# The second up projection of a gated decoder layer as two blocks of seven products, with sums of its weights kept in DRAM

## The chip, the core and the metric

The kernel runs on one core of one Trainium2 chip. Its engines are PE (TensorE, matrix products and transposes), DVE (VectorE), ACT (ScalarE), POOL (GpSimd) and SP (SyncE); each takes its own instructions in order, and they wait for each other by semaphores. DMA transfers are issued here from SP (weights, and the result) and from POOL (everything else); PEld in the profile is the loading of a matmul's stationary operand. The metric is the device time of one execution in microseconds (us), lower is better. All arithmetic is float32. A product of two float32 matrices is made on PE of three passes, by splitting each operand into a high part (a rounded copy, made on ACT) and a low part (operand minus high part, made on DVE): high x high, high x low, low x high.

## The reference, cut to what matters

The sequence has 512 rows, the model 2048 columns. One layer of a decoder trunk:

```python
h = rms_norm(x, norm_g[l])
proj = h @ w_in[l]
q, kv, g_logits, z_a, uv, z_b, merge_logits = jnp.split(proj, SPLIT_IDX, axis=-1)
...
o_a = nsa_attention(q, k_c, v_c, k_s, v_s, k_w, v_w, g_logits, ...) * jax.nn.silu(z_a)
o_b = spatial_gating(uv, ln_v_g[l], ln_v_b[l], sgu_w[l], sgu_b[l]) * jax.nn.silu(z_b)
g_a, g_b = jnp.split(jax.nn.sigmoid(merge_logits), 2, axis=-1)
merged = g_a * (o_a @ w_up_a[l]) + g_b * (o_b @ w_up_b[l])
x = x + merged @ w_out[l]
x = x + jax.nn.sigmoid(x @ w_ple_gate[l]) * (p[l] @ w_ple[l])
return rms_norm(x, final_g)
```

`o_a` and `o_b` are 512 x 1024, `w_up_a` and `w_up_b` are 1024 x 2048. The change is about `o_b @ w_up_b`.

## The kernel before

**Jobs.** Every product with a weight matrix is a `Job` (line 39); the function `gemm` (line 331) runs all jobs in the order in which they were added and hands control back after each small unit of matmuls, so that other work can be put between units (`fill(n)` runs n units, `finish(name)` runs to the end of a job). There are three kinds. "T" has the weights as the stationary operand (four blocks of 128 rows to a piece of weights, 12 matmuls). "N" has the activations as the stationary operand and makes a block of 512 columns from all rows of weights. "S" makes a block of 1024 columns and all 512 rows by seven products of half-size blocks instead of eight (the scheme of Strassen in Winograd's form): the seven products are named 1, 5, 6, 3, 7, 2 and 4, and sums and differences of quarter blocks stand for the operands of 5, 6, 7 and 4 on the weight side, and of 5, 6, 3 and 7 on the activation side. Weight sums are made on DVE in `sum_to` (line 245, the subtract at L258), results are added up in `evac_quad` (line 672): products 1, 5 and 6 are copied out of PSUM by ACT (`keep`), products 3, 7 and 2 are added to these by DVE, product 4 is passed on directly.

**Order of the jobs.** pl0 to pl3; kc0, kc1, vc0, vc1, k00, k01, k10, k11 (kind T, four pieces each), vs (N, 256 columns, eight pieces), vw (N, 304 columns, sixteen pieces), then eight q and eight za jobs around the attention, u, vn, zb (S), the merge gates m0 to m3 (S), ua0 and ua1 (S, `o_a @ w_up_a`), ub0 to ub3 (N, `o_b @ w_up_b`, line 807), wo0, wo1 (N) and wo2 (S), pg0, pg1, pg3.

**Weights on their way.** A piece goes through `load_to` (SP, into a ring of tiles: three for `raw`), a copy on ACT (`hi` or, for kind S, `hs`, 128 x 1024) and a subtract on DVE (`lo` or `ls`), both from `split_to` (line 270), which runs two pieces ahead of PE; the rings of `lo`, `hs` and `ls` have three tiles. At every piece `pop` (line 324) also runs `state["pops"]` steps of the queue `background`, a list of small functions. What has been put into `deferred` is run at the next piece.

**Beside the keys and values.** `h_chunk` (line 455) makes sums of the normalized input and stores them (`hsum`, POOL) from k01 on, half a step per piece. The memory of the ring `b11` (four tiles) is free from kc0 until the first q job takes tiles of it; two of the four hold weights of the compressor for a while.

**Beside the gates.** During m0 to m3 the background queue first finishes a layer norm: `ln_load`, `ln_affine` (two DVE instructions, L1535 and L1536, for each of eight blocks of 128 rows x 512 columns, through DRAM and a pair of tiles `v`), then eight times `group` (line 539): load the operands (`first`, `second`), a spatial product on PE six steps later, its gate on DVE, a transpose on PE (`turn`), a split, and two stores to `ob_dram`.

**The up projections.** ua takes its seven activation operands ("slots", 1 MB each) from DRAM, where `oa_chunk` (line 1386) has stored sums of `o_a` with their high and low parts. Its results go to the tiles `h` of the activation memory. The gate of the first branch is loaded to the tiles `l` (`load_gate_a`) and multiplied in by `gate_a` (DVE, L791) during ub. ub reads `o_b` from two tiles of 2 MB. `evac_up` (line 794) multiplies by the second gate (DVE, L798) and adds the first branch (POOL, L800). `turn_merged` (line 1639) then transposes the merged block on PE, eight transposes at a time, and splits it for the output projection.

Of the kernel before, what the change touches and what calls it, by code (L numbers as in the profile page):

```python
# [37 lines left out]
class Job:  # L38
# [8 lines left out]
    def __init__(self, name, kind, w, c0, cols, kt, act, evac, banks=None, tail=0, c2=None, order=("15", "63", "7", "24")):  # L47
# [3 lines left out]
        self.order = order  # L51
# [13 lines left out]
def kernel(ctx: ExitStack, tc: tile.TileContext, x, p, norm_g, w_in,  # L65
# [59 lines left out]

    def act_part(i, k, sl):
        if isinstance(k, slice):
            return parts_of[i][k.start // 4][:, k.start % 4:k.start % 4 + k.stop - k.start, sl]
        return parts_of[i][k // 4][:, k % 4, sl]
# [50 lines left out]
    def add_job(job):  # L180
        jobs.append(job)
        if job.kind == "S":
            half, c2 = job.kt // 2, job.c2
            ld = {}
            direct = job.order[0] == "1"
# [28 lines left out]
    state = {"loads": 0, "sum": 0, "high": 0, "low": 0, "ahead": 0, "more": 1, "pops": 2, "due": 0, "b11": 0}  # L214
# [30 lines left out]
    def sum_to(i):  # L245

        while state["sum"] <= min(i, len(subs) - 1):
            job, p, j, ld = subs[state["sum"]]
            if job.kind != "S" or p not in "5674":
                state["sum"] += 1  # L250
                continue
# [8 lines left out]
    def source(i):  # L260
        job, k, n, ld = subs[i]
        if job.kind == "S":
# [60 lines left out]

    def pop():
        state["due"] += state["pops"]
# [207 lines left out]
    def evac_q(ft):  # L533
        def f(ps):
            pair = ring((0, 3, 2)[ft % 3], F32R)
# [71 lines left out]
    ob_dram = dram.tile([P, 2, 8, S], F32R, name="ob_d")  # L607
# [140 lines left out]
    def ob_act(k):  # L748
        return ob_h[:, k], ob_l[:, k]

    oa_slot = {}

    def oa_act(p, k, t):
        return (oa_slot[p][:, i, k, t * P:t * P + P] for i in range(2))
# [13 lines left out]
    up_tiles = {}  # L768

# [6 lines left out]
    def load_gate_b(cg):  # L776
        up_tiles[cg] = new_s4(cg - 1, F32) if cg in (1, 2) else new_x()
        nc.gpsimd.dma_start(up_tiles[cg], gate_columns(1, cg))
# [15 lines left out]
    def evac_up(cg):  # L794
        def e(ps):
            g = up_tiles[cg]
            for t in range(TT):
                nc.vector.scalar_tensor_tensor(out=g[:, t], in0=g[:, t], scalar=1.0, in1=ps[t],  # L798
                                               op0=ALU.add, op1=ALU.mult)
                nc.gpsimd.tensor_tensor(out=g[:, t], in0=g[:, t], in1=parts_of["h"][cg][:, t], op=ALU.add)  # L800
        return e

    for i in range(2):
        add_job(Job(f"ua{i}", "S", w_up_a, 1024 * i, 512, 8, oa_act, evac_quad(None, lambda t, c, i=i: place_up_a(t, 1024 * i + c)),
                    (("o", "t", "s"), ("g", "t", "s"))[i]))
    for cg in range(4):
        add_job(Job(f"ub{cg}", "N", w_up_b, 512 * cg, 512, 8, ob_act, evac_up(cg), (ys, xs)[cg % 2]))
# [207 lines left out]
    quad["ring"] = ph_r.enter_context(tc.tile_pool(name="ring", bufs=1))  # L1015
    mid = ph_ab.enter_context(tc.tile_pool(name="mid", bufs=1))
# [369 lines left out]
    def oa_chunk(c):  # L1386

        w = {}

        def load():  # L1390
            for n, f in (("1", c), ("2", c + 4)):
                w[n] = mix["pool"].tile([P, S], F32, tag="v", name="oa_f", bufs=2)
                nc.gpsimd.dma_start(w[n], o32_dram[:, f])

        def put(n, tags, places, sl=slice(0, 512)):

            def f():
                width = sl.stop - sl.start
                h = mix["pool"].tile([P, S], F32R, tag=tags[0], name="oa_" + tags[0])
                if len(tags) == 2:  # L1400
                    l = mix["pool"].tile([P, S], F32R, tag=tags[1], name="oa_" + tags[1])
                else:
                    l = w[n].bitcast(F32R) if width == 512 else h[:, 256:]
                high(h[:, :width], w[n][:, sl], 0.5)

                def rest():
                    low(h[:, :width], l[:, :width], w[n][:, sl], 0.5)
                    for j, i in enumerate(places):
                        for a, o in enumerate((h, l)):
                            nc.gpsimd.dma_start(oa_dram[:, i, a, c], o[:, 256 * j:256 * j + 256])  # L1410
# [8 lines left out]
        def sums_24():  # L1419
            f1, f2 = w["1"], w["2"]  # L1420
            sub(f1[:, lo_t], f2[:, hi_t], f1[:, lo_t])
            sub(f2[:, lo_t], f2[:, lo_t], f1[:, lo_t])

# [81 lines left out]
    def load_s3():  # L1505
        for q in range(2):
# [126 lines left out]
    for cg in range(3):  # L1633
        load_gate_b(cg)
# [236 lines left out]
```

## Time and profile before

| | us |
|---|---|
| median of three runs | 1551.98 (1551.78 to 1552.4) |
| the profiled execution, its own time | 1551.81 |
| its span, first to last instruction | 1550.1 |
| PE busy | 1536.1 (99%) |
| DVE busy | 1194.6 (77%) |
| ACT busy | 785.4 (51%) |
| POOL busy | 251.4 (16%) |

| Stage | from, to (us) | length |
|---|---|---|
| keys and values, kc0 to vw | 32.3 to 181.4 | 149.1 |
| gates m0 to m3 | 720.0 to 1036.1 | 316.1 |
| ua | 1036.1 to 1112.3 | 76.2 |
| ub, with three of four `turn_merged` | 1112.3 to 1204.7 | 92.4 |

How to read the profile: it is one execution as the hardware profiler recorded it. A row of a group gives line, engine, operation, the names it writes and reads, shapes, count, then busy us and mean ns of one, then the idle time before it and what ended that. A row of the timeline gives start, duration, engine, line, operation, and in brackets the idle time before it and its releaser. In the list of waits a row gives the waiting instruction, the one that released it, us in total, times, and the longest. The rows themselves stand in the prediction.

### The profile page before, as it was taken

The page shows a single profiled execution, that of the slowest core. Times are in us where ns is not written, and L with a number is a line of the kernel's source. Part 1 is how long each engine was busy: PE and PEld are TensorE (multiplying, and loading weights), DVE is VectorE, ACT ScalarE, POOL GpSimd, SP SyncE. Part 2 cuts the span into 40 slices and gives each one's busy share as a digit, 9 for nine tenths or more (in the row PEclk, how much of TensorE's full clock was granted, in tenths as well). Part 3 has the DMA queues.
Part 4 walks back from the last instruction along what each step waited for, and adds up shares of the span by engine and source line. Part 5 has one row for each costly group of instructions (what it writes and reads, how often), then busy time and mean ns, then how long its engine had stood idle before and what let it go on. Part 6 is the DMA issues. An engine that isn't in the chain of part 4 may idle for free.

```text
span 1550.1 us, 20517 instructions
## 1 busy us (share of the span) xinstructions
PE 1536.1 (99%) x7438; PEld 1287.8 (83%) x7438; DVE 1194.6 (77%) x1869; ACT 785.4 (51%) x1345; POOL 251.4 (16%) x413
## 2 busy tenths in 40 slices
PE   9999999999999999999999999999999999999997
PEld 7889988888888888888888888888888888888886
DVE  7547758888886888978887777777666587888877
ACT  6434446666675555545545444455423344544556
POOL 1201101101122242201121212210131221000000
PEclk9999999999999999999999999999999999999999
DMA  8436722123226895826473737674743497464655
GB/s 322 129 82 195 224 71 59 49 61 107 78 69 212 251 294 133 265 69 230 144 258 116 262 104 254 233 259 175 289 132 96 120 278 228 150 203 165 189 202 192
DMA packets 161429, 269.23 MB, mean 174 GB/s; under 512 B 9752, under 2 KB 80048, under 8 KB 158768
## 3 DMA queue, kind: packets, MB, share of 16 engines
q1 hardware_dynamic: 116240, 151.67, 31.1%
q0 software_dynamic: 44944, 116.00, 22.3%
q8 instruction: 58, 0.95, 0.2%
q14 instruction: 43, 0.35, 0.1%
q10 hardware_dynamic: 144, 0.26, 0.0%
HBM read 209.69 MB, written 58.20 MB: 173 GB/s over the span
## 4 chain that ended last, share of the span: by engine, by line
PE 96%; DVE 2%; ACT 1%; issue 0%; POOL 0%; DVEq 0%; POOLq 0%; ACTq 0%
PE ps_m L355 7%; PE ps_m L357 7%; PE ps_m L356 7%; PE ps_za L381 2%; PE ps_t L1204 2%; PE ps_za L382 2%; PE ps_za L383 2%; PE ps_ub L393 2%; PE ps_ub L394 2%; PE ps_wo L394 2%; PE ps_ub L395 2%; PE ps_wo L395 2%; PE ps_wo L393 2%; PE ps_wo L356 2%; PE ps_wo L355 2%; PE ps_pg L356 2%
## 5 line engine op out<-in xcount | busy, mean ns | idle before, releaser
L148 DVE TENSOR_TENSOR ls<-b,hs 128x1024 fp32r<-128x1024 f32 x196 | 239.7, 1224 | 116.1 <-ACT hs L142 115.0
L142 ACT CAST hs<-b 128x1024 fp32r<-128x1024 f32 x196 | 206.1, 1052 | 231.3 <-PE ps_m L357 88.0
L148 DVE TENSOR_TENSOR lo<-raw,hi 128x512 fp32r<-128x512 f32 (+1 forms) x216 | 151.6, 706 | 81.8 <-issue 26.1
L142 ACT CAST hi<-raw 128x512 fp32r<-128x512 f32 (+1 forms) x216 | 129.3, 606 | 138.6 <-PE ps_ub L395 48.5
L142 ACT CAST hs<-raw 128x1024 fp32r<-128x1024 f32 x80 | 84.2, 1054 | 98.4 <-PE ps_m L357 35.5
L148 DVE TENSOR_TENSOR ls<-raw,hs 128x1024 fp32r<-128x1024 f32 x80 | 97.8, 1222 | 17.2 <-ACT hs L142 17.0
L355 PE MATMUL ps_m<-hs,act_h 128*128 128x512 f32 x256 | 100.5, 393 | 0.0
L356 PE MATMUL ps_m<-ls,act_h 128*128 128x512 f32 x256 | 99.7, 389 | 0.0
L357 PE MATMUL ps_m<-hs,act_l 128*128 128x512 f32 x256 | 99.7, 389 | 0.0
L258 DVE TENSOR_TENSOR b<-raw,b 128x1024 f32<-128x1024 f32 x80 | 97.5, 1218 | 1.6 <-DMA raw<-in_w_in_dram 1.6
L258 DVE TENSOR_TENSOR b<-b,b 128x1024 f32<-128x1024 f32 x80 | 97.5, 1218 | 0.0
L142 ACT CAST pth<-ps_t 128x512 fp32r<-128x512 f32 (+1 forms) x88 | 48.0, 545 | 65.8 <-PE ps_t L1204 65.4
L1165 ACT ACTIVATE prob<-prob,st 128x512 f32<-128x512 f32 (+3 forms) x128 | 70.7, 556 | 4.0 <-DVE st L1156 3.8
L148 DVE TENSOR_TENSOR ptl<-ps_t,pth 128x512 fp32r<-128x512 f32 (+1 forms) x88 | 56.2, 639 | 21.0 <-ACT pth L142 20.0
L1156 DVE CUSTOM_DVE_ANT_0 prob<-ps_s,b 128x512 f32<-128x512 f32 (+3 forms) x128 | 56.3, 486 | 9.9 <-PE ps_s L1153 9.7
L357 PEld LDWEIGHTS ps_m<-hs,act_l 128*128 128x128 f32 x256 | 48.1, 188 | 10.1
L356 PEld LDWEIGHTS ps_m<-ls,act_h 128*128 128x128 f32 x256 | 48.1, 188 | 9.7
L355 PEld LDWEIGHTS ps_m<-hs,act_h 128*128 128x128 f32 x256 | 48.1, 188 | 9.7
L381 PE MATMUL ps_za<-act_h,hi 128*128 128x512 f32 x128 | 55.7, 435 | 0.0
L381 PE MATMUL ps_q<-act_h,hi 128*128 128x512 f32 x128 | 53.6, 419 | 0.0
L1204 PEld LDWEIGHTS ps_t<-ident,prob 128*128 128x128 f32 x320 | 39.7, 140 | 13.8 <-DVE ptl L148 2.8
L1204 PE MATMUL ps_t<-ident,prob 128*128 128x128 f32 x320 | 49.5, 273 | 1.4 <-DVE ptl L148 1.3
(641 smaller groups left out, 4391.3 us busy)
## 6 DMA issues: line engine op xcount, KB each, us to landing
raw<-in_w_in_dram SPq DMA_DIRECT2D x112, 512.0 KB, 3.8
b<-in_w_in_dram SPq DMA_DIRECT2D x56, 512.0 KB, 5.8
raw<-in_w_out_dram SPq DMA_DIRECT2D x24, 512.0 KB, 4.1
raw<-in_w_ple_gate_dram SPq DMA_DIRECT2D x24, 512.0 KB, 3.9
raw<-in_w_up_b_dram SPq DMA_DIRECT2D x16, 512.0 KB, 3.7
hsum<-h_stage POOLq DMA_DIRECT2D x12, 512.0 KB, 4.0
gate<-keep POOLq DMA_DIRECT2D x24, 256.0 KB, 4.1
oa_d<-oa_g POOLq DMA_DIRECT2D x40, 128.0 KB, 3.1
```

Of the source, the lines that this page charges most:

```text
L142: nc.scalar.copy(hi, src)
L148: nc.vector.tensor_tensor(out=lo, in0=src, in1=hi.bitcast(F32), op=ALU.subtract)
L258: nc.vector.tensor_tensor(out=b[o], in0=b[x], in1=b[y], op=ALU.subtract)
L355: nc.tensor.matmul(o, ah, wh, start=st, stop=False, skip_group_check=go)
L356: nc.tensor.matmul(o, ah, wl, start=False, stop=False, skip_group_check=go)
L357: nc.tensor.matmul(o, al, wh, start=False, stop=sp, skip_group_check=go)
L381: nc.tensor.matmul(ps, hi[:, j], ah, start=st, stop=False)
L393: nc.tensor.matmul(o, ah[:, sl], hi[:, j], start=st, stop=False)
L394: nc.tensor.matmul(o, ah[:, sl], lo[:, j], start=False, stop=False)
L395: nc.tensor.matmul(o, al[:, sl], hi[:, j], start=False, stop=sp)
L1165: nc.scalar.activation(sl, sl, AF.Exp, bias=st[:, 0, j, hh:hh + 1], scale=-1.0, accum_out=st[:, 1, j, hh:hh + 1])
L1204: nc.tensor.transpose(b[:, (2 * e + hh) * P:(2 * e + hh + 1) * P], pts[hh][:, c:c + P], ident)
```

## The change

The four ub jobs become two of kind S of 1024 columns each. Unlike the other jobs of this kind, their weight sums are not made while they run: a new argument `sums` names four DRAM tensors for each block, and every product loads its own weights (`raw`, 512 KB for two blocks of 128 rows).

```diff
+            if job.sums:
+                for p, j in products(job):
+                    c, k = {"1": (job.c0, 0), "2": (job.c0, half), "3": (c2, half)}.get(p, (0, 0))
+                    src = weights(job, k + 2 * j, 2, c) if p in "123" else job.sums[p][:, 2 * j:2 * j + 2]
+                    ld[p, j] = add_load("raw", src, 2, job.cols)
+                    last_sub[ld[p, j]] = len(subs)
+                    subs.append((job, p, j, ld))
+                return
...
-    for cg in range(4):
-        add_job(Job(f"ub{cg}", "N", w_up_b, 512 * cg, 512, 8, ob_act, evac_up(cg), (ys, xs)[cg % 2]))
+    for i in range(2):
+        add_job(Job(f"ub{i}", "S", w_up_b, 1024 * i, 512, 8, slot_act(ob_slot), evac_quad(final_up(i), tiles=False),
+                    (("o", "t", "s"), ("g", "t", "s"))[i], sums=up_sums[i]))
```

The sums are made in eight sets of five steps from kc1 on, in two tiles of the ring `b11`. `pop` runs 0.85 of a step of this new queue `slow` for every piece, ahead of the background's.

```diff
     def pop():
+        state["late"] += 0.85
+        if state["late"] >= 1:
+            state["late"] -= 1
+            if slow:
+                slow.popleft()()
...
+    ab, cd = (ring(i, F32) for i in range(2))
+    def up_set(i, k):
+        a, b, c, d = ab[:, 0], ab[:, 1], cd[:, 0], cd[:, 1]
+        def minus(o, x, y, p):
+            nc.vector.tensor_tensor(out=o, in0=x, in1=y, op=ALU.subtract)
+            nc.gpsimd.dma_start(up_sums[i][p][:, k], o)
+        def load():
+            for o, f, col in ((a, k, 0), (b, k, 512), (c, k + 4, 512), (d, k + 4, 0)):
+                nc.gpsimd.dma_start(o, w_up_b[f * P:f * P + P, 1024 * i + col:1024 * i + col + 512])
+        def first():
+            minus(b, b, a, "5")
+            minus(c, c, b, "6")
+        def second():
+            minus(a, c, a, "7")
+            minus(d, d, c, "4")
+        return [load, lambda: None, first, second, lambda: None]
+    for i in range(2):
+        for k in range(4):
+            slow.extend(up_set(i, k))
```

Beside the gates, `o_b` is now prepared as `o_a` was: two groups make a pair, ACT copies each transposed group to a tile, and then sums of the two are made, split and stored in 14 transfers of 128 KB a pair (`put`, moved out of `oa_chunk` into `put_steps`). The background runs at 1.42 steps a product instead of 1.

```diff
+    def group_pair(c):
+        both = {}
+        put, sums_13, sums_24 = put_steps(both, c, ob_dram, None)
+        def sums_put():
+            sums_24()
+            put("1", ("g0",), (2, 4))()
+        return (group(c, both) + group(c + 4, both) + [nothing, put("2", ("g0", "g1"), (5, 6)), nothing, nothing,
+                put("1", ("v",), (0,), lo_t), sums_13, sums_put, nothing, put("2", ("g1",), (3, 1)), nothing])
...
-    for g in range(8):
-        background.extend(group(g))
-    state["pops"] = 1
+    for c in range(4):
+        background.extend(group_pair(c))
+    state["pops"] = 1.42
```

In the up projections the first gate of columns 0 to 1023 is multiplied in during ua1, that of the others during ub0; seven slots of 1 MB are loaded for ub, five in ua1 and two at its end; the second gate goes to the tiles `l`. The merged block stays in the tiles `h`, and `turn_merged` runs once for two blocks of 512 columns, the second of them first; its results take the places of gates and merged columns that are done with, in pairs of 128 rows that a new table `pair_of` finds again.

```diff
+    def final_up(i):
+        def f(t, c, o, src):
+            cg = 2 * i + c // 512
+            g, m = (parts_of[n][cg][:, t] for n in "lh")
+            nc.vector.scalar_tensor_tensor(out=g, in0=g, scalar=1.0, in1=src, op0=ALU.add, op1=ALU.mult)
+            nc.gpsimd.tensor_tensor(out=m, in0=m, in1=g, op=ALU.add)
+        return f
...
+    state["pops"] = 1
+    gates_a((0, 1))
     load_gate_a(2)
     fill(4 * 4)
-    nc.gpsimd.dma_start(ob_h, ob_dram[:, 0])
+    for i in range(2):
+        load_ob(i, ob_h[:, 4 * i:4 * i + 4])
+    load_gate_a(3)
     fill(4 * 4)
-    nc.gpsimd.dma_start(ob_l, ob_dram[:, 1])
-    load_gate_a(3)
+    for i in range(2):
+        load_ob(2 + i, ob_l[:, 4 * i:4 * i + 4])
+    fill(4 * 2)
+    load_ob(4, new_s4(0))
     finish("ua1")
+    load_ob(5, new_s4(1))
+    load_ob(6, new_x(F32R))
+    gates_a((2, 3))
+    for cg in range(2):
         load_gate_b(cg)
...
+    finish("ub0")
+    assert not background
+    for cg in range(2, 4):
+        load_gate_b(cg)
+    fill(8)
+    turn_merged(0, "oo", 6)
+    finish("ub1")
+    fill(4)
+    turn_merged(1, "gs", 4)
```

Outside of these, four loads of `s3_dram` become eight of half the size.

147 lines of the change are left out of this document (74 added, 73 removed).

## The prediction

> **What bounds the kernel now.** I read the page first (span, engines, slices, chain), then the list of who waited on PE, then busy time by stage, then the order of single instructions where the change adds work.
>
> ```profile
> span 1550.1 us, 20517 instructions
> PE 1536.1 (99%) x7438; PEld 1287.8 (83%) x7438; DVE 1194.6 (77%) x1869; ACT 785.4 (51%) x1345; POOL 251.4 (16%) x413
> ...
> PE 96%; DVE 2%; ACT 1%; issue 0%; POOL 0%; DVEq 0%; POOLq 0%; ACTq 0%
> ...
> PE ps_spin L947 <- POOL eps_t L87: 1.4, 1, 1.4
> PE ps_t L1204 <- DVE ptl L148: 1.3, 1, 1.3
> ```
>
> PE is busy for 99% of the span, holds 96% of the chain, and its two longest waits are 1.4 and 1.3 us. So a matmul taken away shortens the kernel by the spacing of matmuls, and a microsecond for which PE is made to wait lengthens it by as much. The spacing comes from the stages. The columns after the length are busy us (instructions) of PE, PEld, DVE, ACT, POOL, then clock, DMA share, GB/s; the rows are ua, ub, the gates m0 to m3, the keys from k00 on, vs, vw, and three pieces of m0.
>
> ```profile
> 1036.10:1112.30 76.20, 76.20 (x338) 63.10 (x337) 57.85 (x57) 38.70 (x48) 6.79 (x11) 1.00 0.61 221
> 1112.30:1204.70 92.40, 92.40 (x434) 77.05 (x433) 55.02 (x73) 26.70 (x46) 21.86 (x17) 1.00 0.42 138
> 720.00:1036.00 316.00, 315.99 (x1441) 262.44 (x1441) 252.32 (x250) 154.38 (x180) 62.48 (x106) 1.00 0.60 200
> 80.80:131.90 51.10, 51.10 (x251) 42.92 (x251) 30.56 (x55) 22.11 (x40) 1.68 (x4) 1.00 0.39 113
> 131.90:154.90 23.00, 23.00 (x193) 22.99 (x192) 17.20 (x29) 9.70 (x20) 2.65 (x5) 1.00 0.64 190
> 154.90:181.40 26.50, 26.50 (x194) 26.50 (x193) 22.83 (x42) 12.86 (x28) 4.26 (x8) 1.00 0.76 222
> ...
> 720.00:740.00 20.00, 20.00 (x90) 16.54 (x90) 18.50 (x23) 11.96 (x16) 5.37 (x10) 1.00 0.45 153
> 740.00:760.00 20.00, 20.00 (x90) 16.58 (x89) 17.08 (x18) 9.27 (x10) 4.20 (x8) 1.00 0.48 148
> 760.00:780.00 20.00, 20.00 (x90) 16.57 (x89) 18.62 (x21) 11.82 (x14) 2.53 (x6) 1.00 0.63 208
> ...
> L1645 PE MATMUL ps_m<-ident,s 128*128 128x128 f32 x32 | 4.1, 272 | 0.0
> L1645 PE MATMUL ps_m<-ident,x 128*128 128x128 f32 x16 | 2.1, 272 | 0.0
> ...
> 1145.99 0.87 PE ps_m L1645 x8
> ```
>
> ua has the new form of product already: 2 blocks of 7 products of 24 matmuls are 336 in 76.2 us, 0.2268 us each. ub's 384 would take 87.1 us at that spacing, and its six groups of eight transposes 6 x 0.88 = 5.3; the sum is the 92.4 us measured. So ub has no stall to give back, and the duration of 0.39 us that the page shows for one matmul is not its price.
>
> **1. The products.** ub becomes 2 x 7 x 24 = 336 matmuls of the same shape. 48 fewer x 0.2268 = **-10.9 us**. The 64 transposes stay, in eight groups as before.
>
> **2. The sums of the weights, beside keys and values.** Eight sets, each of four loads, four subtracts on DVE and four stores of 256 KB, are issued step by step: 0.85 step for each weight piece, five steps to a set (load, nothing, two subtracts, two subtracts, nothing). 40 steps take 47 pieces, from kc1 into vw. A piece lasts 2.72 us for keys (12 matmuls) and 1.65 in vw (26.5 / 16).
>
> ```profile
> 108.11 0.69 DVE L438 TENSOR_TENSOR h_b<-act_h,act_l 128x512 f32<-128x512 f32 x1
> 108.72 0.69 DVE L438 TENSOR_TENSOR h_a<-act_h,act_l 128x512 f32<-128x512 f32 x1
> ...
> 125.99 0.69 DVE L148 TENSOR_TENSOR lo<-raw,hi 128x512 fp32r<-128x512 f32 x1
> ...
> 171.66 0.47 DVE L148 TENSOR_TENSOR lo<-raw,hi 128x304 fp32r<-128x304 f32 x1
> ...
> 126.74 0.50 PE L383 MATMUL ps_k<-act_h,lo 128*128 128x512 f32 x1
> ...
> 174.92 0.30 PE L394 MATMUL ps_vw<-lo,act_h 128*128 128x304 f32 x1
> ...
> DMA to landing us min/median/max: 2.3/3.0/7.2
> ...
> oa_f<-o_d POOLq DMA_DIRECT2D x8, 256.0 KB, 3.6
> ```
>
> A subtract of this shape takes 0.61 to 0.69 us (starts 0.61 apart), so 32 of them are some 20 us of DVE. From 80.8 to 181.4 DVE is busy 70.6 of 100.6 us, so on average they fit. What counts is DVE's lead: the split-off low part of a piece must be ready when PE comes to it. In vw the part ready at 172.13 is used at 174.92 at the latest, a lead of 2.7 us; at 126.68 one is ready as PE asks for it, and that matmul takes 0.50 us: the lead there is nil already.
>
> The new wait: a subtract waits for its loads, the loads wait on POOL until the set before is stored. By the rows for 256 KB (the first line is the landing of the o_d transfers, min/median/max) that chain is 3.0 for the store, two POOL issues of 0.55, and 3.6 for the load: 7.7 us. Four steps lie between, 4.7 pieces: 12.8 us in the keys, where it is covered, but 7.8 in vw, of which the other subtract takes 0.65. So in vw each of two sets comes late by 0.5 us at medians, and by some 2 more where POOL must first issue an hsum store that waits for DVE, and where the DMA share of 0.76 is raised: a set moves 2.1 MB in 9.8 us, 214 GB/s on top of 222. DVE has 3.7 us idle in vw and gets four pairs, 5.2 us. Queued behind a waiting subtract are the low parts of the next pieces, and PE waits for those. Two sets x (2.5 late + 0.75 of work that does not fit) less the lead of 2.7 is 3.8 us; with 0.7 for the places without lead, **+4.5 us**. From below, 0.5 (the lead covers vw); a gain is excluded, as nothing is removed here. From above, the chain at the longest landings, 7.2 + 1.1 + 7.2 = 15.5 us: priced under the rivals. I take the value near the medians because both transfers have rows of their own size.
>
> **3. Beside the gates.** Per pair of groups of ob DVE gets 1.5 more splits (0.68) and four half-size sums (half of 0.69), 2.4 us; four pairs make 9.7 us on 252.3 of 316 (83% after). ACT's 3.5 more copies a pair and POOL's 40 more stores (0.54 each, 21.6 us) lie on engines busy 154 and 62 of 316. The background runs at 1.42 steps a product instead of 1. That squeezes the layer norm's eight row blocks (1.5 us each, L1535 and L1536) from 26 products into 18, where DVE is already busy 54.2 of 60 us: 12 us of work over 50 instead of 71 raises 90% to about 97%.
>
> ```profile
> 741.99 0.75 DVE L1535 SCALAR_TENSOR_TENSOR v<-v,small,lg 128x512 f32<-128x512 f32 x1
> 742.77 0.75 DVE L1536 SCALAR_TENSOR_TENSOR v<-v,small,lg 128x512 f32<-128x512 f32 x1
> ...
> 746.85 0.54 POOL L1531 DMA_DIRECT2D v<-vn_d  x1 [2.48 <-DMA vl_d<-v]
> ...
> v<-vn_d POOLq DMA_DIRECT2D x8, 256.0 KB, 5.5
> mix_u<-u_d POOLq DMA_DIRECT2D x8, 256.0 KB, 4.7
> ```
>
> A block's buffer comes back by store and load: 741.99 to 746.85, plus 5.5, is 10.4 us; five steps are now 3.5 products, 9.6 us. DVE so waits 0.8 us for the last block of each half, inside a lead of some 3 us (below). **+0.5 us**, from 0 to 3. The operands of the spatial product have 4.2 products (11.5 us) instead of 16.3 to land, against 4.7 and three issues; between pairs a store goes ahead, about 3 us more. No charge; PE would stand behind it directly, up to 3 us.
>
> **4. The ub stage itself.** DVE: 32 low parts of 0.69 go, 28 of 1.22 and 12 sums of 0.64 come, eight gate products of ua move to ua1: 55.0 - 22.1 + 34.2 + 7.7 - 7.1 = 68 of 81.5 us, 83%; the gates run at 80% without a wait of PE.
>
> ```profile
> 1100.01 1.22 DVE L148 TENSOR_TENSOR ls<-b,hs 128x1024 fp32r<-128x1024 f32 x1 [0.31 <-ACT hs L142]
> ...
> 1104.35 0.39 PE L356 MATMUL ps_ua<-ls,x 128*128 128x512 f32 x1
> ...
> raw<-in_w_up_b_dram SPq DMA_DIRECT2D x16, 512.0 KB, 3.7
> b<-in_w_up_a_dram SPq DMA_DIRECT2D x8, 512.0 KB, 8.2
> ...
> L800 POOL TENSOR_TENSOR s<-s,act_h 128x512 f32<-128x512 f32 x8 | 11.9, 1514 | 26.0 <-DVE s L798 26.0
> ...
> 1040.00:1060.00 20.00, 20.00 (x90) 16.58 (x89) 14.96 (x15) 10.72 (x14) 1.60 (x3) 1.00 0.98 371
> ```
>
> The lead in this form is 3.1 us (ready 1101.23, used 1104.35). SP loads 28 pieces of 512 KB, one per 2.72 us, instead of 16. A ring of three gives each about two products plus the lead, 5.8 + 3.1 = 8.9 us, against landings of 3.7, or 8.2 under load. In ub0 come two slots and two gates besides, some 300 GB/s; 371 ran in ua without a stall. POOL's seven slot loads wait in order for PE to leave ua's slots, and the third and fourth gate load stands behind them, needed a job later. After ub1 four POOL adds (6.1 us) end near 7.8 us; the first transposes, after 2.7 us, use the other columns, and those that need the adds come after 9.9. DVE's low parts wait there for the gate tile, about 3.4 us, ahead of a weight piece that PE wants 10.8 us after ub1. **+0.3 us**, from 0 to 3.4.
>
> **Sum.** -10.9 + 4.5 + 0.5 + 0.3 = -5.6 us on the profiled execution: its span of 1550.1 becomes 1544.5, its time of 1551.81 becomes 1546.2. The median of the runs lies 0.17 higher, so I forecast **1546.3 us**.
>
> **Rivals.** (a) All of the new work is hidden: 1551.98 - 10.9 = 1541.1. For it: 30% of DVE is idle beside the keys; against it, the lead of nil at 126.7 and the 0.5 us by which the chain misses in vw even at medians. Chance 0.13.
>
> (b) Slower: the chain of store, issue and load in the keys and values. At 15.5 us vw would lose 2 x (15.5 - 7.15) - 2.7 = 14 us, and five sets in the keys and vs 3.3 us each, less some 2 of lead, 6.5; 1541.1 + 20.5 = 1561.6. It eats the gain from a chain of about 14 us: 2 x (14 - 7.15) - 2.7 = 11. For it: the longest landing, 7.2. Against it: the medians are half of that and most sets run where the DMA share is 0.39 to 0.64. Chance 0.11.
>
> (c) The weight stream in ub is late: landings like 10.8 (two 1 MB gate loads beside 8.2 for the weights) would cost some 2 us at three or four pieces, so 6 more than the forecast: 1552. Against it: ua at 371 GB/s. Chance 0.09. The Trainium skill, DMA: Bandwidth & Descriptors, section "Queues, rings and completion order", says that each DMA engine takes turns between the queues that have work, packet by packet. By that rule SP would keep half of 371 GB/s, 186, beside POOL's four transfers of 1 MB, where the weights need 193 (512 KB in 2.72 us): less than 1 us behind after the 23 us that those 4 MB take, inside the lead, and (c) rarer still.
>
> (d) Waits of PE that lower its clock.
>
> ```profile
> 1540.00:1550.00 10.00, 0.49 (x3) 0.07 (x1) 4.62 (x9) 3.79 (x7) 0.00 (x0) 0.77 0.55 210
> ```
>
> In the last 10 us PE works for 0.49 and the granted clock has a mean of 0.77, so it falls when PE stands still; at half speed that is 4.6 us, a loss of 2.3 us had there been matmuls. Two such falls after waits in vw would add 4.6: 1550.9. Against it: every wait estimated above is under 3 us, and the waits of 1.4 us now cost no clock. Chance 0.05. The Trainium skill, TensorE: Matmul & The Clock Gate, section "Why this matters for your kernels", warns against idle gaps of PE of more than about 3 us, after which the clock goes to half; the row of the last 10 us agrees, and by that rule the waits in vw would stay just short of it.
>
> **How the numbers follow.** The forecast, waits of 2 to 8 us in all (1543 to 1549), has 0.62; (a) 0.13, (c) 0.09, (d) 0.05, (b) 0.11. 0.2% of the time, 3.1 us, is what can be told from no change: faster is under 1548.9, slower over 1555.1. Faster: (a) and nearly all of the forecast, 0.73; same: the rest of it, (c), (d), 0.16; slower: (b), 0.11. The range runs from (a) to just over (c), 1540.8 to 1553.
>
> **What would show it.** 7390 matmuls instead of 7438, ub some 10.9 us shorter with PE still at spacing 0.2268; waits of PE on low parts between 120 and 185 us of 3 to 6 us in all, most of them in vw, with DVE released by the landing of w_up_b. Wrong would be: waits of over 1 us in ub or the gates, no wait before 185 us (a), or several of over 2 us there (b).

## The result, and the profile after

| | before | after |
|---|---|---|
| median of the runs, us | 1551.95 (1551.78 to 1552.4, 4 runs) | 1564.68 (1564.28 to 1566.14, 4 runs) |
| span of the profiled execution, us | 1550.1 | 1562.9 |
| start to the first matmul of za | 203.2 | 220.9 (+17.7) |
| from there to the first of ub | 909.1 | 909.9 (+0.8) |
| ub, to the first matmul of wo | 92.4 | 84.6 (-7.8) |
| wo to the end | 345.4 | 347.5 (+2.1) |

The ratio is 1.0083 (95%: 1.0066 to 1.0101): slower by 12.7 us, where a gain of 5.6 us had been forecast. The stages add up to the 12.8 us by which the span grew. The first place to look is the stretch up to za. It holds keys, values and the first q job, and in it PE has the same matmuls as before.

A line of the page after with the busy times, then two of its DMA issues (count, KB each, median us from issue to landing):

```profile
PE 1535.5 (98%) x7390; PEld 1283.2 (82%) x7390; DVE 1244.4 (80%) x1933; ACT 805.8 (52%) x1369; POOL 317.8 (20%) x526
...
b<-in_w_up_b_dram POOLq DMA_DIRECT2D x32, 256.0 KB, 6.0
t<-b POOLq DMA_DIRECT2D x32, 256.0 KB, 3.7
```

7390 matmuls, 48 fewer, as forecast; the loads of the sums land in 6.0 us and their stores in 3.7, where the forecast had taken 3.6 and 3.0. The list of waits after (waiting instruction, releaser, us in total, times, longest):

```profile
PE ps_vw L416 <- DVE lo L153: 6.9, 2, 4.7
PE ps_ub L378 <- DVE ls L153: 2.3, 4, 1.0
PE ps_k L405 <- DVE lo L153: 2.1, 1, 2.1
...
PE ps_q L405 <- DVE lo L153: 1.1, 1, 1.1
...
DVE b L1041 <- DMA b<-in_w_up_b_dram: 16.6, 7, 5.2
```

PE waits for low parts, at two places in vw, one in the keys, one in q; DVE, which makes them, waits 16.6 us for the loads of the sums. These PE waits on low parts ahead of za are 10.1 us of the 17.7. Windows of the timeline show most of the rest (length, then busy us and count of PE, PEld, DVE, ACT, POOL, then clock, DMA share, GB/s):

```profile
130.00:135.00 5.00, 5.00 (x16) 3.92 (x16) 4.56 (x8) 1.66 (x3) 0.00 (x0) 0.66 1.04 368
170.00:175.00 5.00, 4.00 (x17) 3.77 (x17) 4.96 (x10) 1.93 (x4) 2.41 (x5) 0.66 0.79 257
185.00:190.00 5.00, 2.45 (x10) 2.45 (x11) 4.24 (x8) 0.00 (x0) 2.17 (x4) 0.51 0.64 219
190.00:195.00 5.00, 5.00 (x31) 5.00 (x31) 4.66 (x10) 3.43 (x7) 1.08 (x2) 0.81 0.93 266
```

Behind each longer wait the granted clock is low for a while. PE's busy time times what the clock lacks, summed over the four rows (1.7 + 1.4 + 1.2 + 0.9), is an estimate of 5.2 us. The chain itself, for the eighth set in vw, DVE's rows and then POOL's:

```profile
171.46 0.68 DVE L1041 TENSOR_TENSOR b<-b 128x512 f32<-128x512 f32 x1
...
179.70 0.47 DVE L153 TENSOR_TENSOR lo<-raw,hi 128x304 fp32r<-128x304 f32 x1
185.32 0.69 DVE L1041 TENSOR_TENSOR b<-b 128x512 f32<-128x512 f32 x1 [5.15 <-DMA b<-in_w_up_b_dram]
```

```profile
171.84 1.14 POOL L1042 DMA_DIRECT2D t<-b  x2 [0.45 <-DVE b L1041]
174.75 0.54 POOL L488 DMA_DIRECT2D hsum<-h_stage  x1 [1.77 <-DVE h_stage L153]
177.19 0.55 POOL L488 DMA_DIRECT2D h_d<-h_stage  x1 [1.90 <-DVE lo L153]
178.06 2.15 POOL L1046 DMA_DIRECT2D b<-in_w_up_b_dram  x4 [0.33 <-issue]
```

The seventh set's last subtract is done at 172.1. POOL has issued its last two stores at 173.0, then has to issue two stores of the h sums, each of which waits for DVE, and comes to the eighth set's loads at 178.06. How long the two stores (`t`, 171.8 to 173 us) and the first two of these loads (`b`, to 178.9 us) took to land:

```profile
DMA to landing us min/median/max: 5.6/5.6/5.6
```
```profile
DMA to landing us min/median/max: 5.5/6.1/6.6
```

So the stores landed at 177.4 and 178.0, just before POOL came to the loads: the h sums ahead of them in its order cost 0.6 us at most. The second load, which the first subtract needs, landed at 185.3; DVE has stood at the subtract for 5.15 us, no low part is made after 180.2, and PE waits 4.7. From subtract to subtract the chain took 13 us. The seventh set's loads, at 161.9, waited 2.25 us for stores that took 5.8 and 5.9 to land.

### The profile page after: what moved, and what is told of

It is laid out like the page before. It is cut to its first block, busy times and chain, and to the rows that moved or that the text cites. A ratio compares the mean times of both kernels' runs of the same rounds, so it can differ in the third digit from the quotient of the medians.

```text
span 1562.9 us, 20745 instructions
## 1 busy us (share of the span) xinstructions
PE 1535.5 (98%) x7390; PEld 1283.2 (82%) x7390; DVE 1244.4 (80%) x1933; ACT 805.8 (52%) x1369; POOL 317.8 (20%) x526
## 4 chain that ended last, share of the span: by engine, by line
PE 83%; DVE 5%; DMA 5%; issue 3%; ACT 2%; POOL 1%; DVEq 0%; POOLq 0%; ACTq 0%
PE ps_m L378 6%; PE ps_m L379 6%; PE ps_m L377 6%; PE ps_za L403 2%; PE ps_t L1248 2%; PE ps_za L404 2%; PE ps_za L405 2%; PE ps_wo L416 2%; PE ps_wo L417 2%; PE ps_wo L415 2%; PE ps_pg L378 2%; PE ps_wo L378 2%; PE ps_zb L378 2%; PE ps_vn L379 2%; PE ps_zb L379 2%
## 5 line engine op out<-in xcount | busy, mean ns | idle before, releaser
L147 ACT CAST hs<-raw 128x1024 fp32r<-128x1024 f32 x108 | 113.6, 1054 | 130.3 <-PE ps_m L379 28.2
L153 DVE TENSOR_TENSOR ls<-raw,hs 128x1024 fp32r<-128x1024 f32 x108 | 139.2, 1290 | 36.2 <-ACT hs L147 36.1
L153 DVE TENSOR_TENSOR lo<-raw,hi 128x512 fp32r<-128x512 f32 (+1 forms) x184 | 125.6, 688 | 43.6 <-issue 17.0
L147 ACT CAST hi<-raw 128x512 fp32r<-128x512 f32 (+1 forms) x184 | 108.3, 603 | 84.2 <-PE ps_wo L417 19.4
L405 PE MATMUL ps_q<-act_h,lo 128*128 128x512 f32 x128 | 50.3, 393 | 1.1 <-DVE lo L153 1.1
## 6 DMA issues: line engine op xcount, KB each, us to landing
act_l<-gate POOLq DMA_DIRECT2D x8, 1024.0 KB, 11.7
```

Source lines behind the costliest of these rows:

```text
L147: nc.scalar.copy(hi, src)
L153: nc.vector.tensor_tensor(out=lo, in0=src, in1=hi.bitcast(F32), op=ALU.subtract)
L405: nc.tensor.matmul(ps, lo[:, j], ah, start=False, stop=sp)
```

## The experiments

"Loss" is the start of za less the 203.2 us of before, so it takes in the first q job; "q" is the same for the start of that job, 181.4 us before. "ub" runs from its first matmul to wo's first. If nothing in ub were late, it would be 336 matmuls x 0.2268 and four groups of eight transposes x 0.88, 79.7 us. The ratio is against runs of the kernel before on the same chip, with its 95% interval; those have medians of 1551.74 to 1551.95 us.

| run | us | ratio | loss | q | ub |
|---|---|---|---|---|---|
| the change | 1564.68 | 1.0083 (1.0066 to 1.0101) | 17.7 | 16.4 | 84.6 |
| e1_ub_only | 1548.3 | 0.9977 (0.9968 to 0.9986) | 0.0 | 0.0 | 84.1 |
| e2_no_loads | 1551.51 | 1.0001 (0.9991 to 1.001) | 6.1 | 3.9 | 82.9 |
| e3_no_subtracts | 1553.9 | 1.0016 (1.0007 to 1.0026) | 9.0 | 2.0 | 84.3 |
| e4_ub_dve | 1551.6 | 0.9998 (0.9989 to 1.0008) | 0.0 | 0.0 | 88.3 |
| e5_kv_buffers | 1558.54 | 1.0043 (1.0028 to 1.0058) | 13.3 | 11.7 | 84.8 |
| e6_dve_adds | 1565.66 | 1.0086 (1.0069 to 1.0103) | 18.0 | 18.0 | 86.3 |
| e7_half_sums | 1548.86 | 0.9983 (0.9973 to 0.9992) | 3.6 | 3.6 | 82.9 |
| e8_buffers_adds | 1560.28 | 1.0054 (1.0039 to 1.0069) | 13.0 | 11.9 | 85.6 |
| e9_five_places | 1555.65 | 1.0026 (1.0017 to 1.0036) | 9.0 | 7.0 | 85.2 |
| e10_half_early | 1547.51 | 0.9971 (0.9959 to 0.9983) | 2.8 | 2.8 | 82.8 |
| e11_half_early_turn | 1549.29 | 0.9981 (0.9972 to 0.9991) | 3.1 | 3.1 | 84.0 |
| e12_no_gates | 1561.65 | 1.0063 (1.0048 to 1.0078) | 17.9 | 16.6 | 81.2 |
| e13_places_no_subtracts | 1553.4 | 1.0008 (0.9998 to 1.0017) | 6.4 | 2.9 | 84.1 |
| e14_half_first | 1546.46 | 0.9964 (0.9951 to 0.9978) | 1.4 | 1.4 | 82.8 |

The loss is read from rows like these, before and after (min/median/max ns, then first and last start):

```profile
L381 PE MATMUL ps_za<-act_h,hi x128: 389/397/796, 203.2 to 488.9; 128*128 128x512 f32 x128
```
```profile
L403 PE MATMUL ps_za<-act_h,hi x128: 389/397/796, 220.9 to 506.6; 128*128 128x512 f32 x128
```

### The new form of ub without the sums beside the keys

```diff
-                    src = weights(job, k + 2 * j, 2, c) if p in "123" else job.sums[p][:, 2 * j:2 * j + 2]
+                    src = weights(job, k + 2 * j, 2, c)
...
-    for i in range(2):
-        for k in range(4):
-            slow.extend(up_set(i, k))
```

> Leaves out the forming of the weight sums beside the keys and values (no load, no subtract, no store); in the second up projection the pieces that held sums are loaded from the weights themselves, so the loads, matmuls and everything after them keep their number and size. Theory (the keys and values lost 17.8 us to the chain of store, load and subtract, the second up projection 4.9 us of its own, the gates under 1): q starts near 181 us of the span as before the change, the second up projection still takes 84 to 85 us, and the time is 1564.7 - 17.7 = about 1547. Rival (the loss beside the keys comes from other parts of the change, such as the slower rate of the background or the changed order of buffers): time stays above 1555. Rival for the second up projection (its stall is late lag carried over from the keys or sums' own 4 KB rows): it takes 80 us and the time is near 1542.

Loss nil, 1548.3 us: the whole loss belongs to the sums beside the keys, and ub's own stall (84.1 instead of 79.7) is no echo of it.

### Loads or subtracts taken away

```diff
-        return [load, lambda: None, first, second, lambda: None]
+        return [load if (i, k) == (0, 0) else lambda: None, lambda: None, first, second, lambda: None]
```

> Leaves out seven of the eight sets of loads of the weights for the sums: all 32 subtracts and 32 stores run, on the four tiles that the first set loaded. Theory (DVE stands at subtracts until the loads land, and the low parts behind them come late): the waits of DVE on these loads (16.6 us in all after the change) are gone, q starts at 182 to 185 us instead of 197.8, time 1549 to 1552. Rival A (DVE has no room for 20 us of subtracts): q still starts later than 192 us, time over 1559. Rival B (the stores alone hold POOL and the buffers): DVE waits at subtracts for stores instead, in all over 8 us, time over 1556.

Loss 6.1: 11.6 us of the 17.7 come and go with the loads. The time, 1551.51 us, is as expected; q starts at 185.3, just past the 182 to 185. The list of waits, 60 to 215 us:

```profile
DVE b L1041 <- DMA b<-in_w_up_b_dram: 4.6, 2, 4.3
...
PE ps_k L405 <- DVE lo L153: 2.1, 1, 2.1
```

4.6 us of DVE's wait belong to the one set that is still loaded. The PE wait of 2.1 in the keys, at 130 us, is there although nothing but that set is loaded, and it is gone in the next run, which subtracts nothing: it is DVE's work. Rival B shows nowhere: DVE waits for no store.

```diff
-            nc.vector.tensor_tensor(out=o, in0=x, in1=y, op=ALU.subtract)
             nc.gpsimd.dma_start(up_sums[i][p][:, k], o)
```

> Leaves out the 32 subtracts: the four loads and four stores of each set run as before, and the stored tiles are the loaded weights. Theory (DVE's in-order wait is what hurts): with no subtract DVE never waits for these transfers, q starts at 181.5 to 184 us, time 1547 to 1550, although all 16.8 MB of loads and 16.8 MB... of that order of stores still move. Rival (the transfers take DMA share and HBM from the weights of the keys and values, so the weight pieces themselves land late): q starts later than 190 us with ACT's high parts waiting for the weights, time over 1556.

(What moves is 32 loads and 32 stores of 256 KB, 8.4 MB each way; the figure in the expectation is too high.) Loss 9.0, and the time, 1553.9 us, lies between the two. q starts at 183.4, as the theory had it; the other 7.0 us are lost in the first q job, where PE waits for high and low parts. DVE does not wait for the sums here, but ACT waits for buffers of the h sums (30 to 215 us):

```profile
POOL t L1041 <- DMA b<-in_w_up_b_dram: 33.5, 14, 4.8
...
POOL b L1045 <- DMA t<-b: 23.0, 7, 6.0
...
ACT h_stage L147 <- DMA hsum<-h_stage: 12.5, 4, 4.6
```

POOL stands 33.5 us at stores whose loads have not landed and 23.0 at loads whose tiles are still being stored; the stores of the h sums are queued behind, their three buffers come back late, and ACT, in order, makes the weights' high parts late. So the transfers hurt without DVE too, either by POOL's order or by the DMA engines they fill.

### Buffers of their own

From the fourth set on, free tiles (two of the ring that the compressor has left, and `o32`), loads one set ahead:

```diff
+    def up_load(i, k):
+        if (i, k) in loaded:
+            return
+        t = places.popleft() if places else (ab, cd)
...
+        return [lambda: up_load(i, k), ahead, first, second, ahead]
...
+    places.extend([tuple(ring(i, F32) for i in (2, 3)), (o32[:, 0:2], o32[:, 2:4]), (o32[:, 4:6], o32[:, 6:8]), (ab, cd)])
```

> The changed kernel with more buffers for the sums: from the fifth set on, each set has four tiles of its own (those that the compressor has left, and the attention's output tile, idle until then), and its loads are issued one set ahead, so that no load waits for a store and no subtract for a fresh load. All 32 loads, subtracts and stores stay. Theory (the single set of buffers makes a chain store, issue, load, and both DVE and POOL's queue stand in it in order): DVE's waits on these loads fall from 16.6 us to under 4, q starts at 183 to 187 us instead of 197.8, time 1549 to 1554. Rival (8.4 MB in and 8.4 MB out beside keys and values fill the DMA engines, so weights and sums both land late whatever the buffers): q starts later than 192 us, time over 1557.

Loss 13.3; time and start of q are as the rival had them. But the places were handed out from the fourth set on, not from the fifth as the expectation says, so four of them were one too few, and the eighth set went back to the old way. One row of POOL and the windows:

```profile
172.58 2.16 POOL L1043 DMA_DIRECT2D b<-in_w_up_b_dram  x4 [0.43 <-issue]
```
```profile
175.00:180.00 5.00, 2.54 (x19) 2.30 (x17) 0.00 (x0) 0.45 (x1) 0.28 (x1) 1.00 0.93 266
180.00:185.00 5.00, 1.78 (x7) 1.78 (x8) 3.58 (x6) 0.00 (x0) 1.96 (x4) 0.51 0.55 196
```

One late set: DVE idle for a whole window, 5.7 us of idle PE (2.46 + 3.22), and a clock of 0.51 after it. With a place for the eighth set as well:

```diff
+    places.append(places[0])
```

> As the run with buffers of their own, which gave out one set too early: there the last set's loads were issued at its own turn, 172.6 us, and DVE then waited 6.2 us for them. Here the eighth set too has a place and its loads go one set ahead. Theory (what is left of the loss is 2.3 us near 130 us, where DVE is full of subtracts and h sums and waits for no transfer, some 1 us each at 66 us for the first loads and near 200 us): the wait of 5.7 us in vw and the lower clock after it (3.4 us) go, q starts at 184 to 187 us, time 1548.5 to 1552. Rival (DMA share of about 1 from 155 us on: any order of loads only moves the wait): q starts later than 190 us, time over 1555.

That wait is gone, but the loss is 9.0: q starts at 188.4 instead of 184 to 187, and the time, 1555.65 us, is the rival's. In this run the DMA share is 0.88 to 1.11 in each 5 us from 155 to 195. Whether it is order or share was put to the same kernel without the subtracts:

> As the run with a place for every set from the fourth on and loads one set ahead, but without the 32 subtracts (leaves out forming the sums): transfers alone, without the chain of store and load. Without subtracts and with the chain the loss up to u was 9.2 us. Theory (that loss came from POOL's order: loads waiting for stores and stores for loads held back the stores of the h sums behind them, so that their three buffers came back late to ACT): without that order q and the first gates lose under 3 us, time 1548.5 to 1551. Rival (the transfers themselves fill the DMA engines and make the h sums' stores and the weights land at 6 to 7 us instead of 4): the loss stays at 7 to 10 us, time 1554 to 1557.5.

Loss 6.4 (e3: 9.0), time 1553.4 us: between the two. Places of their own and the early loads are worth 2.6 us here. The rest was not split further: the transfers fill the DMA engines, but POOL, too, still stands 14.7 us at stores whose loads have not landed. Two rows, of the waits (30 to 215 us) and of the DMA issues (100 to 215 us):

```profile
ACT hi L147 <- DMA raw<-in_w_in_dram: 19.8, 8, 5.3
```
```profile
raw<-in_w_in_dram SPq DMA_DIRECT2D x8, 304.0 KB, 8.1
```

ACT now waits 19.8 us for the weights of the keys and values: vw's pieces land in 8.1 us. Before the change, and in the change, the same view says:

```profile
raw<-in_w_in_dram SPq DMA_DIRECT2D x15, 512.0 KB, 3.7
...
raw<-in_w_in_dram SPq DMA_DIRECT2D x8, 304.0 KB, 3.9
```
```profile
raw<-in_w_in_dram SPq DMA_DIRECT2D x13, 512.0 KB, 5.5
...
t<-b POOLq DMA_DIRECT2D x22, 256.0 KB, 3.5
b<-in_w_up_b_dram POOLq DMA_DIRECT2D x20, 256.0 KB, 6.4
raw<-in_w_in_dram SPq DMA_DIRECT2D x8, 304.0 KB, 5.3
```

The weights land later because of what was added. The parts do not add up: 6.1 without loads and 6.4 of transfers alone, 9.0 with both and buffers of their own, 17.7 on one set of buffers. So doing away with the chain on one set of buffers is worth 8.7 us (e9).

### Half of the sums

```diff
-                    (("o", "t", "s"), ("g", "t", "s"))[i], sums=up_sums[i]))
+                    (("o", "t", "s"), ("g", "t", "s"))[i], sums=up_sums[1] if i else None))
...
-    for i in range(2):
-        for k in range(4):
-            slow.extend(up_set(i, k))
+    for k in range(4):
+        slow.extend(up_set(1, k))
```

> Half of the change: only the four sets for the second half of the second up projection are made beside keys and values (all before the sixth key piece of the second pair, at the same pace); the first half has its sums formed by DVE as the first up projection has. Theory (the loss beside the keys comes with sets five to eight, where they meet the h sums on DVE and POOL, and in the short pieces of vw): q starts at 182 to 183.5 us, the second up projection takes 82 to 86 us, time 1547 to 1552. Rival (each set costs about the same, 17.8 / 8 = 2.2 us): q starts near 190 us, time over 1555.

Loss 3.6 of 17.7 for half the sets, with q at 185.0 instead of 182 to 183.5; the time, 1548.86 us, is as expected. PE waits for low parts for 0.9 us in vc, at 66 us, behind the first set's loads (below), and for 2.2 at 130. DVE's rows about the second place begin with the fourth set's subtracts (L1041) and end with the lows of k (L535):

```profile
115.92 0.69 DVE L1041 TENSOR_TENSOR b<-b 128x512 f32<-128x512 f32 x1
...
128.23 1.39 DVE L535 TENSOR_TENSOR ob_l<-ps_k,ob_h 64x512 fp32r<-64x512 f32 x2 [1.70 <-ACT ob_h L531]
```

From 113.9 to 126.5 DVE has no gap. The h sum (L460) that it starts at 120.8 us in e1 starts at 124.5 here (1.3 of it is lost before). ACT copies that sum and only then k, from 125.8 instead of 122.2; DVE's lows of k wait for these copies, the next low part stands behind them, and PE waits for that. No wait for a transfer is in it. Then the four sets were moved out of the way:

```diff
-        state["late"] += 0.85
-        if state["late"] >= 1:
+        state["late"] += 1.2
+        while state["late"] >= 1:
...
+    slow.insert(1, slow[1])
+    slow.insert(1, slow[1])
```

> As the run with four sets beside the keys and DVE's own sums for the first half, but at 1.2 steps a piece instead of 0.85 and with two more empty steps after the first load: all four sets are then done before the h sums begin, and the first subtract comes later than its loads. Theory (the loss of 3.5 us there is 1.1 us for the first loads and 2.3 us for the fourth set's subtracts among the first h sums): q starts at 181.4 to 182.5 us, time 1545.5 to 1547.5. Rival (the faster pace runs into store, issue, load again, now in the compressor's part): q starts at 184 us or later, time 1548.5 or more.

The time, 1547.51 us, is at the upper end of what was expected, faster than both kernels; q starts at 184.2, as the rival had it. The wait at 130 is gone, the one at 66 is not, and one of about 1.3 us at 81 is new, where the compressor's own splits are now among the subtracts. DVE and POOL about the first loads:

```profile
61.65 0.69 DVE L1041 TENSOR_TENSOR b<-b 128x512 f32<-128x512 f32 x1 [4.79 <-DMA b<-in_w_up_b_dram]
```
```profile
58.97 0.54 POOL L1046 DMA_DIRECT2D b<-in_w_up_b_dram  x1 [2.43 <-DMA o<-in_cmp_w_k_dram]
```

DVE waits 4.8 us for them; the last of the four was issued behind a wait for the compressor's weights. Issued ahead of these (the edit is against that run):

```diff
-    slow.insert(1, slow[1])
-    slow.insert(1, slow[1])
+    slow.popleft()()
+    for _ in range(3):
+        slow.appendleft(lambda: None)
```

> As the fastest run so far (four sets at 1.2 steps a piece), with the first set's four loads issued on POOL ahead of the compressor's weights instead of behind them; its subtracts stay at the same place. Theory (PE's wait of 1.1 us near 66 us is DVE's wait of 4.8 us for these loads): DVE's wait goes, q starts at 182.5 to 183.5 us instead of 184.3, time 1546 to 1547. Rival (the loads land no earlier, or the compressor's weights now come late and cost the same): q at 184 us or later, time 1547.5 or more.

```profile
DVE b L1041 <- DMA b<-in_w_up_b_dram: 0.7, 1, 0.7
```

The wait is gone and with it PE's at 66 us. The loss is 1.4 us, most of it the other wait (1.15 us, now at 80), and the time 1546.46 us, 5.3 us under the kernel before. The intervals of this run and of e10 overlap; the trace tells them apart.

### ub's own stall

DVE forming all sums of ub, as it does for ua:

```diff
-                    (("o", "t", "s"), ("g", "t", "s"))[i], sums=up_sums[i]))
+                    (("o", "t", "s"), ("g", "t", "s"))[i]))
```

> Undoes one part of the change: no sums beside keys and values and none in DRAM; the second up projection keeps its seven products, but DVE forms the sums as it does for the first up projection, from 16 loaded pieces instead of 28. DVE's work in the second up projection by the rows of the first: 28 low parts of 1.22 (34.2), 16 sums of some 1.2 (19.7), 12 half sums of 0.64 (7.7), 16 gate products of 0.75 (12), low parts of transposes 5.5, 79 of 79.7 us. Theory (PE loses only what DVE's overload makes): q at 181.5, that stage 80 to 86 us, time 1542 to 1548, faster than both kernels. Rival (DVE at about 100% and in order makes PE wait at every product, with the clock falling): stage over 90 us, time over 1552.

No faster than before: ub takes 88.3, between theory and rival. Its worst place is the end of the first half, where DVE is full (5.00 of 5.00) with four instructions, and PE idles 4.3 us:

```profile
1160.00:1165.00 5.00, 0.66 (x4) 0.35 (x3) 5.00 (x4) 2.03 (x3) 5.00 (x4) 1.00 0.00 0
```

POOL's adds run beside. Whether they are the cause of such a stall was asked in the changed kernel, by giving them to DVE:

```diff
-            nc.gpsimd.tensor_tensor(out=m, in0=m, in1=g, op=ALU.add)
+            nc.vector.tensor_tensor(out=m, in0=m, in1=g, op=ALU.add)
```

> The changed kernel with the 16 adds of the second up projection on DVE instead of POOL. Theory (a POOL add of 1.95 us and a DVE low part beside it hold each other up, so that an add costs DVE about 1 us, more than the 0.64 us of doing it itself): the low parts there take 1.22 us throughout, the second up projection falls from 84.6 to 82.5 to 83.5 us, time 1562.5 to 1563.7. Rival A (the adds are not the cause of that stall; DVE only gets 10 us more): the stage is as long or longer, time 1564.5 to 1567. Rival B (all of its stall comes from the late weight pieces at its start): no change, 1564.7.

ub is longer by 1.7 us, as rival A had it. The low parts do take 1.22 us again, but the adds, 0.69 each, now stand in DVE's order ahead of them and of the reads of PSUM (L719). PE waits 1.65 us, to 1166.6, while the two L719 run (1165.8 to 1167.1); that it waits for this bank is argued from the order of the rows, not shown. On top of the own buffers the adds likewise gave nothing:

> Both: the sums with buffers of their own from the fifth set on, and the 16 adds on DVE. Theory: the two gains add, q starts at 183 to 187 us, second up projection 82.5 to 83.5 us, time 1547 to 1552.5. Rival: with DVE as the engine that is late in both places, the adds give nothing, time as with the buffers alone.

Nor did a later transposition (`fill(8)` to `fill(14)` ahead of `turn_merged(0, ...)`), which made ub 1.2 us longer than in e10 and PE's wait there 2.53 us instead of 1.64:

> As the run before, and the transposes of the first half's result are issued six steps (4 us) later. Theory (PE's wait of about 2 us at the end of the first half comes from final products, adds on POOL and low parts of the transposes falling together): that wait shrinks to under 1 us, time 1 us less than the run before. Rival (the low part that PE waits for stands behind the final products and adds alone): no change.

The start of ub was tested by leaving out the loads of the second gate there (`load_gate_b(0)` and `(1)` dropped):

> The changed kernel without the two loads of 1 MB of the second gate at the start of the second up projection (its first half is multiplied with what stands in these tiles). Theory (at its start seven slots of 0.5 to 1 MB and these gates share the DMA engines with weight pieces of 512 KB every 2.72 us, share 1.03, so that the pieces land late): PE's waits between 1140 and 1155 us, 2.6 us in all, fall under 0.7; the later wait of 1.2 us at the end of its first half stays; time 1562 to 1563. Rival (the weights are late because of their ring of three buffers, whatever runs beside): no change, 1564.7.

ub is 3.4 us shorter, and the time, 1561.65 us, a little under what was expected. The three windows between 1140 and 1155 us, of the change and of this run:

```profile
1140.00:1145.00 5.00, 4.73 (x20) 3.32 (x19) 1.82 (x2) 3.03 (x5) 0.00 (x0) 1.00 1.03 420
1145.00:1150.00 5.00, 4.38 (x19) 3.21 (x18) 3.65 (x4) 2.05 (x4) 0.00 (x0) 1.00 0.85 321
1150.00:1155.00 5.00, 4.24 (x19) 3.15 (x18) 3.37 (x4) 4.01 (x5) 0.00 (x0) 1.00 0.46 146
```
```profile
1140.00:1145.00 5.00, 5.00 (x23) 3.89 (x22) 3.92 (x5) 4.70 (x7) 0.00 (x0) 1.00 0.47 151
1145.00:1150.00 5.00, 5.00 (x24) 4.14 (x23) 3.49 (x5) 2.31 (x3) 0.00 (x0) 1.00 0.74 229
1150.00:1155.00 5.00, 5.00 (x23) 4.14 (x23) 4.56 (x6) 3.00 (x4) 0.00 (x0) 1.00 0.72 211
```

With 2 MB less to load, PE has no idle time there. The weight pieces issued from 1128 to 1158 us land in 4.8 us at the median and 8.9 at most; in the change it is 5.2 and 10.4, and ACT waits for them. What is left of ub's stall is 1.5 us.

## Why the prediction was wrong, point by point

**1. The products, -10.9:** right. 7390 matmuls, and with the two groups of transposes that now come after ub, 79.7 us would be left of ub; e12 comes to 81.2.

**2. The sums beside keys and values, +4.5:** this step failed; it measured 17.7. In vw the mechanism was the one described, with DVE released by the landing of `w_up_b` where it was said to be; three parts of its price were too low.
The durations 3.0 and 3.6 for 256 KB came from other stretches, the stores' from 265 to 495 us with a DMA share of 0.29, the loads' from 516 to 620 with 0.73. In place, with a share of 0.80 from 100 to 200 us in the change (255 GB/s), they were 3.5 and 6.4, and the weights went from 3.7 to 5.5; the stores that the last two sets' loads waited for took 5.6 to 5.9. Rows of 5.5 and 4.7 for loads of the same size stand in the prediction itself, beside the gates.
So the chain took 13 us for the last set, close to the 14 from which the text said the gain is eaten, and not 7.7, to which some 2 had been added for POOL's order and the higher share; the order itself was 0.6 at most.
DVE's own work beside the keys was put at 0.7 us "for the places without lead" and 0.75 a set in vw; with one set loaded instead of eight 6.1 us stay, and the wait at 130 us is DVE's work alone. The average of 70.6 busy of 100.6 us hid that DVE had hardly a gap from 112.6 to 122.9 already, as e1 shows, where this stage is as before.
The clock was kept out of the sum. By the estimate above it took some 5 us.

**3. Beside the gates, +0.5:** near in size; 0.8 from za to ub, with a PE wait of 0.2 in the gates. What the 0.8 consists of was not asked; in e1 and e4 it is 1.7.

**4. ub itself, +0.3:** too low by 4.6. It was costed with ua's stretch at 371 GB/s as proof that the stream holds; ua loads 16 pieces for its sums, ub 28, and two gates come with them. The "some 300 GB/s" of the forecast is a mean over ub0; from 1140 to 1145 us it was 420. A ring of three was to allow a landing of 8.9 us; the longest was 10.4. That was rival (c), and e12 shows that the two gates make 3.4 us of ub's 4.9.

**The rivals.** (b) came near in the number, 1561.6 against 1564.68, but in part by luck. Its 20.5 us were all to come from the chain; of the 17.7 measured, 6.1 stay without seven of the eight sets' loads, and some 5 are clock, which was (d). ub's 4.9 us are mostly (c). The rivals had been kept apart as if each came alone. The rule of the Trainium skill, DMA: Bandwidth & Descriptors, section "Queues, rings and completion order", by which SP would have kept half of the engines and have been less than 1 us behind, would have made (c) rarer; the windows of 1140 to 1155 us do not bear that estimate out, with 1.65 us of idle PE beside POOL's transfers.

## What to carry to other kernels

A transfer that is added to a stretch must be priced with the landing times that the stretch will have with it in, not with a row from another part; and a single set of buffers with store, issue and load in a row needs that whole chain between its turns, including what stands ahead of it in the issuing queue (in e10, the compressor's weights). Whether DVE has room is read from the places where it has no gap, not from its mean. Half of a saving can be worth more than all of it: here the kernel with four sets, made before the h sums begin, and DVE forming the others in ub ran 5.3 us faster than before; with all eight it ran 12.7 slower, with none (e4) as before.

## What the runs showed of the hardware

**The clock after short waits.** The same wait of about 2.15 us of PE at 130 us stands in eight of the runs. In three (the change, e9 and e12) the matmuls after it start 0.43 us apart instead of 0.23 for about 3 us, in the others they don't. In the three the wait ends at 129.77 to 129.96 us, in the five at 130.14 to 130.66; whether that decides it was not tested. The change, and e7:

```profile
129.77 0.50 PE L405 MATMUL ps_k<-act_h,lo 128*128 128x512 f32 x1 [2.15 <-DVE lo L153]
...
131.06 0.63 PE L403 MATMUL ps_k<-act_h,hi 128*128 128x512 f32 x1
131.49 0.63 PE L404 MATMUL ps_k<-act_l,hi 128*128 128x512 f32 x1
```
```profile
130.40 0.50 PE L405 MATMUL ps_k<-act_h,lo 128*128 128x512 f32 x1 [2.17 <-DVE lo L153]
...
131.20 0.39 PE L405 MATMUL ps_k<-act_h,lo 128*128 128x512 f32 x1
131.43 0.40 PE L403 MATMUL ps_k<-act_h,hi 128*128 128x512 f32 x1
```

The Trainium skill, TensorE: Matmul & The Clock Gate, section "Why this matters for your kernels", warns of gaps of more than about 3 us; here 2.15 us did it in some runs, in e13 a wait of 1.69 us at 184 (clock 0.66 from 185 to 190), and the waits over 4 us did it each time.

**POOL's adds and DVE.** In e10, at the end of ub's first half, two final products with PSUM as one operand take 1.27 us (the second beside POOL's adds), two of the same shape with both tensors in SBUF, beside the adds, 3.11:

```profile
1156.99 1.27 DVE L816 SCALAR_TENSOR_TENSOR act_l<-act_l,ps_ub 128x512 f32<-128x512 f32 x2
1158.18 3.11 DVE L816 SCALAR_TENSOR_TENSOR act_l<-act_l,keep 128x512 f32<-128x512 f32 x2
```
```profile
1157.74 6.91 POOL L817 TENSOR_TENSOR act_h<-act_h,act_l 128x512 f32<-128x512 f32 x4 [4.09 <-DVE act_l L816]
```

In the change two reads of PSUM (L719, at 1162.64) take the same 1.27 beside POOL's adds from 1159.96 to 1163.87. So here a DVE instruction of this shape with two SBUF tensors ran at less than half speed beside POOL's adds, and one that reads PSUM did not slow down. The Trainium skill, VectorE: DVE Perf Modes, section "Two Vector instructions with no wait between them", says in passing that DVE's second read interface to SBUF, which the second tensor needs, is shared with GpSimd; the rows agree.
